# Four instead of three seven-product chunks in the first column-block pair of four late stages

## The chip, the cores and the metric

The kernel runs on one core of one Trainium2 chip. The metric is device time in microseconds (us) of one launch. Before the change it is 1014.27 us, the median of three runs (1013.76 to 1014.40).

## What is computed

One pre-norm layer on 256 tokens of width 2048, in float32, and a final norm. All large terms are products of a 256 x 2048 token matrix with a weight matrix that is read from memory once:

```python
h = rms_norm(x, norm_g)
proj = h @ w_in                      # 2048 x 20496, split into q k v o za gif xb zb ga gb
ya = mlstm_branch(...)               # 256 x 2048
yb = rglru_branch(...)               # 256 x 2048
ya, yb = ya @ w_branch_a, yb @ w_branch_b
merged = sigmoid(ga_p) * ya + sigmoid(gb_p) * yb
y = x + merged @ w_out
out = rms_norm(y, final_g)
```

## The kernel before, in words

**Precision.** Every operand is split in two float32r halves, `hi` (a rounded copy made by ScalarE, ACT) and `lo` (what is left, a subtraction by VectorE, DVE). A product of two operands is three matmuls: hi x hi, hi x lo, lo x hi. So each weight chunk that arrives must pass ACT and DVE before TensorE (PE) can use it: `load_chunk` (DMA L133, copy L140, subtraction L141).

**Chunks and pairs.** A weight matrix is cut in column blocks of 512 and in eight k chunks of 256 rows, `kq` 0 to 7; one chunk of one block is 128 x 1024 in SBUF (512 KB). Function `pair` (L171 to L266) computes two column blocks together, each 256 tokens x 512 columns. They stand in two PSUM tiles `acc` of two banks each; the pool for `acc` holds two tiles, so the next pair's first tile takes the place of this pair's first, and its second that of the second. A k chunk of a pair goes one of two ways:

- `plain` (L235): 2 blocks x 2 k tiles x 2 token tiles = 8 products = 24 matmuls with 512 columns. Two ACT copies (L140) and two DVE subtractions (L141), all 128 x 1024.
- `products` (L187): seven products in place of eight, 21 matmuls, by a Winograd scheme. The weight side needs sums: `t1` and `t2`, each by two DVE instructions of 128 x 512 (L199, L200, L203, L204); then four splits (L180, L181): one of 128 x 512 (`b`) and three of 128 x 1024. The token side needs four sums of 128 x 128 blocks, a "form", made once per chunk by `make_form`: L277 (128 x 512, joins hi and lo, left out where the whole value is at hand), L280 to L283 (128 x 128 each), L284 (ACT) and L285 (128 x 512).

Four of the seven products go to four single PSUM banks `aux`, called p1, p5, p7, p6; the other three go straight into the `acc` tiles. After the last products chunk the aux banks are folded into the result tiles `dst`: an ACT copy of p1 (L252), then DVE adds p6 (L253), p7 (L254) and p5 twice (L255, L256). The plain chunks that are still to come follow, those of the first block and then those of the second, and after each block DVE adds its `acc` tile to `dst` (L262), which frees that tile for the next pair.

**Places.** The tables `S_...` name the chunks of a pair that go by `products`, the tables `L_...` the places (0 to 7) at which they come in the sequence. Four late stages consist of two pairs each, p = 0 and p = 1: `WB` (yb times w_branch_b), `GB` and `GA` (the projections gb and ga of h), and `WA` (ya times w_branch_a). In all eight pairs it is chunks 0, 2, 4, at places 0, 2, 4 (1, 3, 5 in the second pair of `WA`). So after the last products chunk of a pair three plain places per block remain (two in the second pair of `WA`). After `WA` the stage `WO` (output projection) follows; its pair already has four products chunks at places 0, 2, 4, 6.

**Order and buffers.** The program is written straight down; a scheduler sorts the instructions of each engine, with `urgent()` marking those of the weight path. On the chip, each engine then goes through its own list in order, and an instruction that waits holds back all behind it. Arriving chunks have six buffers (`raw`), split weights four pairs (`whi`, `wlo`). Forms for `yb` stand in `PT` (slots 0 to 2), that of h chunk 2 in slot 3; those of h chunks 0 and 4 were made earlier in `F0` and `F4`. The form of ya chunk 0 goes to `PT` slot 0 after `WB`, those of ya chunks 2 and 4 to slots 1 and 2, written in the program after `GA`.

Of the kernel before, what the change touches and what calls it, by code (L numbers as in the profile page):

```python
# [10 lines left out]
F32R = mybir.dt.float32r  # L11
# [8 lines left out]
NB = 512  # L20
# [3 lines left out]
EPS = 1e-6  # L24
NEG = -1e30

S_WB, S_GB, S_GA, S_WA = [((0, 2, 4), (0, 2, 4))] * 4
S_OZ = (((4, 0), (2, 4)), ((4,), (1,)), ((4, 0), (2, 5)), ((4, 0), (0, 2)))
S_V = (((4,), (4,)), ((4,), (4,)))
S_WO = (0, 1, 2, 4)  # L30
L_WB, L_GB, L_GA, L_WA = ((0, 2, 4), (0, 2, 4)), ((0, 2, 4), (0, 2, 4)), ((0, 2, 4), (0, 2, 4)), ((0, 2, 4), (1, 3, 5))
L_WO = (0, 2, 4, 6)
H_FORMS = (4, 0)
PLAN = (dict(Y=('c0', '', '', 'c1',),
# [12 lines left out]
def f(ap):  # L47
    return ap.bitcast(F32)
# [3 lines left out]
def hybrid_encoder(ctx: ExitStack, tc: tile.TileContext, x, xt, pk, bif, fg, wg, wi, wr, wa, wb, wo, out):  # L52
# [12 lines left out]
    def name(n):  # L65
        uid[0] += 1
        return f"{n}_{uid[0]}"
# [4 lines left out]
    def sl(tag, dt=F32, cols=4096):  # L72
        return slot.tile([P, cols], dt, tag=tag, name=name("s" + tag))
# [41 lines left out]
    def drain():  # L115
        while queue or any(lanes):
            tick()
        lanes.clear()
# [149 lines left out]
    def halves(t, i):  # L268
        return t[:, i * 1024:i * 1024 + NB], t[:, i * 1024 + NB:(i + 1) * 1024]

    def make_form(fm, full=None, parts=None, temp=None):
        u = xp.rearrange("p a b -> p (a b)") if temp is None else temp
        if full is None:
            full = u[:, NB:2 * NB]
            hi, lo = parts
            v = full if len(hi.shape) == 2 else full.rearrange("p (k s) -> p k s", s=S)
            dve.tensor_add(v, f(hi), f(lo))  # L277
        a11, a21, a12, a22 = [full[:, i * P:(i + 1) * P] for i in range(4)]
        s1, s2, s3, s4 = [u[:, i * P:(i + 1) * P] for i in range(4)]
        dve.tensor_add(s1, a21, a22)  # L280
        dve.tensor_sub(s2, s1, a11)
        dve.tensor_sub(s3, a11, a21)
        dve.tensor_sub(s4, a12, s2)  # L283
        act.copy(fm[0], u[:, :NB])  # L284
        dve.tensor_sub(fm[1], u[:, :NB], f(fm[0]))  # L285
# [604 lines left out]
    yah, yal = Cols([yas["h"]], 4096), Cols([yas["l"]], 4096)  # L890
    ybh, ybl = [], []
    fslot = {}
    fm_t = []

    def form(x, kq, i, **kw):
        fslot[x, kq] = halves(fm_t[0], i)
        make_form(fslot[x, kq], **kw)

    def h_form(kq, i):
        form("h", kq, i, parts=h_parts(kq))  # L900

    def ya_form(kq, i):
        form("a", kq, i, parts=[t(kq * NB, (kq + 1) * NB) for t in (yah, yal)])

    def forms(x):
        return {kq: v for (n, kq), v in fslot.items() if n == x}
# [3 lines left out]

    k_yb, k_h, k_ya = (sorted(set(sum(v, ()))) for v in (S_WB, S_GB + S_GA, S_WA))
    k_h = [kq for kq in k_h if kq not in hf]
    early = [lambda kq=kq, i=i: h_form(kq, i) for kq, i in zip(k_h, (3, 0, 1))]
    early += [lambda kq=kq, i=i: ya_form(kq, i) for kq, i in zip(k_ya[:1], (3, 0, 1)[len(early):])]

    for j in range(4):
        for i in range(2):
            both = half_tr(wi[BLK_ZB + j], i)
            if i == 0:
                zt = hp.tile([P, 2 * NB], F32, tag="zz" if j else "vhi", name=name("zt"))  # L920
                sg = hp.tile([P, 2 * NB], F32, tag="to" if j else "vlo", name=name("sg"))
            fold(zt[:, i * NB:(i + 1) * NB], both)
        act.activation(sg, zt, AF.Silu)
        dve.tensor_mul(sg, sg, hs[:, j * 1024:(j + 1) * 1024])
        ybh.append(sl(f"C{j}", F32R, 1024))
        ybl.append(sl(f"D{j}", F32R, 1024))
        act.copy(ybh[j], sg)
        dve.tensor_sub(ybl[j], sg, f(ybh[j]))
        if j == 0:
            fm_t.append(sl("PT", F32R))  # L930
        if j == 0:
            drain()
        for kq in (2 * j, 2 * j + 1):
            if kq in k_yb:
                form("b", kq, k_yb.index(kq), full=sg[:, (kq % 2) * NB:(kq % 2 + 1) * NB])
        if j == 1:
            early[0]()
    ybh, ybl = Cols(ybh, 1024), Cols(ybl, 1024)
    nb11 = [0]

# [6 lines left out]
    sgv = [sgb[:, j * 1024:(j + 1) * 1024] for j in range(4)]  # L947
    for p in range(2):
        pair((wb[2 * p], wb[2 * p + 1]), ybh, ybl, forms("b"), S_WB[p], sgv[2 * p:2 * p + 2], b11, lambda jj: None, None, L_WB[p])
    for fn in early[1:]:  # L950
        fn()
    for p in range(2):
        gb = [sl(f"D{2 * p + i}", F32, 1024) for i in range(2)]

        def epi_gb(jj, p=p, gb=gb):
            act.activation(gb[jj], gb[jj], AF.Sigmoid)
            dve.tensor_mul(sgv[2 * p + jj], sgv[2 * p + jj], gb[jj])

        pair((wi[BLK_GB + 2 * p], wi[BLK_GB + 2 * p + 1]), hhi, hlo, forms("h"), S_GB[p], gb, b11, epi_gb, None, L_GB[p])
    ga = []  # L960
    for p in range(2):
        ga += [sl(f"C{2 * p + i}", F32, 1024) for i in range(2)]
# [2 lines left out]
            act.activation(ga[2 * p + jj], ga[2 * p + jj], AF.Sigmoid)  # L965

        pair((wi[BLK_GA + 2 * p], wi[BLK_GA + 2 * p + 1]), hhi, hlo, forms("h"), S_GA[p], ga[2 * p:], b11, epi_ga, None, L_GA[p])
    for i, kq in enumerate(k_ya[1:]):
        ya_form(kq, 1 + i)

    m_t = sl("HL", F32R, 8192)
    mh, ml = Cols([m_t[:, :4096]], 4096), Cols([m_t[:, 4096:]], 4096)
# [157 lines left out]
```

## Time and profile before

| | before |
|---|---|
| time, median of three runs | 1014.27 us |
| span of the profiled execution | 1012.2 us |
| PE busy | 1003.0 us (99%) |
| DVE busy | 875.8 us (87%) |
| ACT busy | 628.6 us (62%) |
| mean share of the DMA engines | 58.9% |
| mean granted TensorE clock | 0.998 |

The profile shows one execution, whose span runs from the first to the last instruction; the median of the runs is 2.07 us above that span, and this difference is taken as the time around it. Matmuls overlap in the pipeline: one is listed with 0.39 us, and in a steady row the next starts about 0.227 us later. A DVE row is likewise listed a little longer than its distance to the next. Times on a timeline are us from the start of the span.

### The profile page before, as it was taken

How to read it: one execution, taken by the hardware profiler on the slowest of the kernel's cores; microseconds unless marked ns; L12 is line 12 of the kernel's file. 1: busy time of each engine (PE TensorE's matmuls, PEld its weight loads, DVE VectorE, ACT ScalarE, POOL GpSimd, SP SyncE). 2: the span in 40 equal slices, each digit the busy share in tenths (PEclk: the TensorE clock that was granted, in tenths of full speed). 3: DMA queues.
4: the chain of work that ended last, by engine and by line, in shares of the span. 5: the costliest groups of instructions: out<-in, count | busy, mean ns of one | idle time of the engine just before them, and what ended most of it. 6: DMA issues, size and time to landing. Idle time of an engine off the chain costs nothing.

```text
span 1012.2 us, 13718 instructions
## 1 busy us (share of the span) xinstructions
PE 1003.0 (99%) x5045; PEld 853.2 (84%) x5045; DVE 875.8 (87%) x1167; ACT 628.6 (62%) x825; POOL 18.6 (2%) x37
## 2 busy tenths in 40 slices
PE   9999999999999999999999999999999999999997
PEld 9888988888888888888888888888888888888886
DVE  6687898889769888997697888998898988999996
ACT  7546477756695786667955564655655656455562
POOL 1000000001001000000100000000000000000000
PEclk9999999999999999999999999999999999999999
DMA  9765446565555565657466466666566656568452
GB/s 349 263 208 157 160 153 198 173 213 197 167 190 167 177 197 184 210 167 227 146 199 208 155 208 188 212 212 201 187 216 200 219 177 212 184 217 336 161 200 83
DMA packets 56387, 199.32 MB, mean 197 GB/s; under 512 B 6400, under 2 KB 7424, under 8 KB 55936
## 3 DMA queue, kind: packets, MB, share of 16 engines
q1 hardware_dynamic: 55456, 197.13, 58.9%
q10 hardware_dynamic: 864, 1.32, 0.4%
q8 instruction: 39, 0.64, 0.3%
q14 instruction: 28, 0.23, 0.1%
HBM read 196.33 MB, written 2.10 MB: 196 GB/s over the span
## 4 chain that ended last, share of the span: by engine, by line
PE 97%; DVE 1%; DMA 1%; ACT 0%; issue 0%; ACTq 0%; SPq 0%; DVEq 0%
PE acc L176 17%; PE acc L177 17%; PE acc L174 17%; PE acc L315 16%; PE acc L318 8%; PE aux L176 3%; PE aux L174 3%; PE aux L177 3%; PE aux L855 1%; PE aux L721 1%; PE aux L720 1%; PE aux L719 1%; PE aux L1053 1%; PE aux L1052 1%; PE aux L1051 1%; PE acc L156 1%
## 5 line engine op out<-in xcount | busy, mean ns | idle before, releaser
L140 ACT CAST whi<-raw 128x1024 fp32r<-128x1024 f32 (+1 forms) x284 | 294.8, 1046 | 196.0 <-PE acc L177 99.7
L141 DVE TENSOR_TENSOR wlo<-raw,whi 128x1024 fp32r<-128x1024 f32 (+1 forms) x284 | 341.5, 1213 | 76.2 <-ACT whi L140 74.4
L176 PE MATMUL acc<-wlo,sHL 128*128 128x512 f32 x554 | 215.9, 390 | 0.0
L177 PE MATMUL acc<-whi,sHL 128*128 128x512 f32 x554 | 215.8, 390 | 0.0
L174 PE MATMUL acc<-whi,sHL 128*128 128x512 f32 x554 | 213.3, 390 | 0.0
L315 PE MATMUL acc<-sHL,whi 128*128 128x512 f32 x704 | 175.9, 393 | 0.0
L315 PEld LDWEIGHTS acc<-sHL,whi 128*128 128x128 f32 x704 | 127.4, 189 | 23.5
L174 PEld LDWEIGHTS acc<-whi,sHL 128*128 128x128 f32 x554 | 104.0, 188 | 21.2
L176 PEld LDWEIGHTS acc<-wlo,sHL 128*128 128x128 f32 x554 | 104.1, 188 | 21.0
L177 PEld LDWEIGHTS acc<-whi,sHL 128*128 128x128 f32 x554 | 104.0, 188 | 20.9
L318 PEld LDWEIGHTS acc<-sHL,wlo 128*128 128x128 f32 x704 | 95.3, 190 | 6.0
L180 ACT CAST whi<-t 128x1024 fp32r<-128x1024 f32 x70 | 73.5, 1051 | 42.9 <-PE acc L177 13.9
L318 PE MATMUL acc<-sHL,wlo 128*128 128x256 f32 x704 | 99.0, 283 | 0.0
L181 DVE TENSOR_TENSOR wlo<-t,whi 128x1024 fp32r<-128x1024 f32 x70 | 85.5, 1222 | 9.0 <-ACT whi L180 8.5
L180 ACT CAST whi<-raw 128x1024 fp32r<-128x1024 f32 x37 | 39.0, 1053 | 27.6 <-PE acc L177 16.9
L181 DVE TENSOR_TENSOR wlo<-raw,whi 128x1024 fp32r<-128x1024 f32 x37 | 45.2, 1222 | 8.7 <-ACT whi L180 8.7
L180 ACT CAST b<-raw 128x512 fp32r<-128x512 f32 x28 | 17.4, 621 | 39.2 <-DMA raw<-wi 16.5
L176 PE MATMUL acc<-wlo,sC 128*128 128x512 f32 x92 | 35.9, 390 | 0.4 <-DVE wlo L141 0.4
L176 PE MATMUL acc<-wlo,sA 128*128 128x512 f32 x92 | 36.0, 392 | 0.0
L177 PE MATMUL acc<-whi,sD 128*128 128x512 f32 x92 | 35.8, 389 | 0.0
L177 PE MATMUL acc<-whi,sB 128*128 128x512 f32 x92 | 35.8, 389 | 0.0
L174 PE MATMUL acc<-whi,sC 128*128 128x512 f32 x92 | 35.3, 389 | 0.0
(361 smaller groups left out, 1589.1 us busy)
## 6 DMA issues: line engine op xcount, KB each, us to landing
raw<-wi SPq DMA_DIRECT2D x254, 512.0 KB, 4.2
raw<-wb SPq DMA_DIRECT2D x32, 512.0 KB, 4.1
raw<-wa SPq DMA_DIRECT2D x32, 512.0 KB, 4.0
raw<-wo SPq DMA_DIRECT2D x32, 512.0 KB, 4.8
raw<-wr SPq DMA_DIRECT2D x8, 512.0 KB, 4.0
sB<-x SPq DMA_DIRECT2D x4, 512.0 KB, 7.7
sA<-x SPq DMA_DIRECT2D x1, 2048.0 KB, 7.9
sA<-xt SPq DMA_DIRECT2D x7, 256.0 KB, 6.7
```

The costliest lines, as they stand in the source:

```text
L140: last_copy[0] = act.copy(hi[:, r], raw[:, r]).ins
L141: last_sub[0] = dve.tensor_sub(lo[:, r], raw[:, r], f(hi[:, r])).ins
L156: pe.matmul(ps[tb], a, wl, start=False, stop=False)
L174: pe.matmul(ps, a, wh, start=id(ps) not in began, stop=False)
L176: pe.matmul(ps, a, wl, start=False, stop=False)
L177: pe.matmul(ps, b, wh, start=False, stop=stop)
L180: act.copy(hi, v)
L181: dve.tensor_sub(lo, v, f(hi))
L315: pe.matmul(ps[m], hi[:, o:o + P], hl_t[:, 2 * k * S:2 * (k + 1) * S], start=(k == 0), stop=(turn and k == KT - 1), skip_group_check=True)
L318: pe.matmul(ps[m][:, :S], lo[:, o:o + P], hhi(k * S, (k + 1) * S), start=False, stop=(not turn and k == KT - 1), skip_group_check=True)
L719: pe.matmul(dst, whi[:, o:o + P], xh[:, r], start=True, stop=False)
L720: pe.matmul(dst, whi[:, o:o + P], xl[:, r], start=False, stop=False)
```

## The change

The first pair of each of the four stages gets a fourth products chunk, `kq` 6, at place 6. Only place 7 is left behind it. The token side then needs forms of chunk 6 of yb, h and ya, and the forms move: yb takes all four `PT` slots; both h forms (chunks 2 and 6) are written after `WB`, into slots 0 and 1; ya chunks 0 and 2 after the first and second pair of `GB`, into slots 2 and 3; ya chunks 4 and 6 after `GA`, into `F0` and `F4`. The early calls in the zb stage go. The host packs chunk 6 of those pairs as it packs the other products chunks.

```diff
-S_WB, S_GB, S_GA, S_WA = [((0, 2, 4), (0, 2, 4))] * 4
+S_WB, S_GB, S_GA, S_WA = [((0, 2, 4, 6), (0, 2, 4))] * 4
...
-L_WB, L_GB, L_GA, L_WA = ((0, 2, 4), (0, 2, 4)), ((0, 2, 4), (0, 2, 4)), ((0, 2, 4), (0, 2, 4)), ((0, 2, 4), (1, 3, 5))
+L_WB, L_GB, L_GA = [((0, 2, 4, 6), (0, 2, 4))] * 3
+L_WA = ((0, 2, 4, 6), (1, 3, 5))
...
-    early = [lambda kq=kq, i=i: h_form(kq, i) for kq, i in zip(k_h, (3, 0, 1))]
-    early += [lambda kq=kq, i=i: ya_form(kq, i) for kq, i in zip(k_ya[:1], (3, 0, 1)[len(early):])]
...
-        if j == 1:
-            early[0]()
...
-    for fn in early[1:]:
-        fn()
+    for i, kq in enumerate(k_h):
+        h_form(kq, i)
...
         pair((wi[BLK_GB + 2 * p], wi[BLK_GB + 2 * p + 1]), hhi, hlo, forms("h"), S_GB[p], gb, b11, epi_gb, None, L_GB[p])
+        ya_form(k_ya[p], 2 + p)
...
-    for i, kq in enumerate(k_ya[1:]):
-        ya_form(kq, 1 + i)
+    for kq, slot_ in zip(k_ya[2:], H_FORMS[::-1]):
+        fslot["a", kq] = halves(sl(f"F{slot_}", F32R, 1024), 0)
+        make_form(fslot["a", kq], parts=[t(kq * NB, (kq + 1) * NB) for t in (yah, yal)])
```

The scheduler's new order is shown at one boundary, that from the first to the second pair of `WB`; the other three have the same shape. Line numbers are one higher in the changed kernel here (L253 there is L252 before). The names: `sE` is the result tile of `WB`, `aux_...` are the banks p1, p5, p7, p6, `wlo` split weights, `t` the weight sums, `b` the split of 128 x 512, `raw` arrived chunks. DVE before, from the second fold (L254) on; the first fold, L253 on `aux_5588` (bank p6), and one L141 stand just ahead of it:

```order
L254 TENSOR_TENSOR sE_5557<-aux_5587,sE_5557 128x512
L141 TENSOR_TENSOR wlo_5817<-raw_5815,whi_5816 128x1024
L255 TENSOR_TENSOR sE_5557<-aux_5586,sE_5557 128x512
L256 TENSOR_TENSOR sE_5557<-aux_5586,sE_5557 128x512
L141 TENSOR_TENSOR wlo_5836<-raw_5834,whi_5835 128x1024
L199 TENSOR_TENSOR t_5898<-raw_5891 128x512
L181 TENSOR_TENSOR b_1260_5895<-raw_5891,b_1260_5895 128x512
L200 TENSOR_TENSOR t_5898<-raw_5892,raw_5891 128x512
L141 TENSOR_TENSOR wlo_5854<-raw_5852,whi_5853 128x1024
L203 TENSOR_TENSOR t_5899<-t_5898,raw_5891 128x512
L141 TENSOR_TENSOR wlo_5872<-raw_5870,whi_5871 128x1024
L204 TENSOR_TENSOR t_5899<-raw_5892,t_5899 128x512
```

The next instruction is the first `acc` addition, L262 on `acc_5558`. DVE in the changed kernel, up to the first `acc` addition; the first fold, L254 on `aux_5587` (bank p6), and one L205 stand just ahead of the piece:

```order
L182 TENSOR_TENSOR wlo_5912<-t_5907,whi_5911 128x1024
L255 TENSOR_TENSOR sE_5556<-aux_5586,sE_5556 128x512
L182 TENSOR_TENSOR b_1288_5990<-raw_5986,b_1288_5990 128x512
L200 TENSOR_TENSOR t_5993<-raw_5986 128x512
L201 TENSOR_TENSOR t_5993<-raw_5987,raw_5986 128x512
L182 TENSOR_TENSOR wlo_5918<-t_5908,whi_5917 128x1024
L256 TENSOR_TENSOR sE_5556<-aux_5585,sE_5556 128x512
L257 TENSOR_TENSOR sE_5556<-aux_5585,sE_5556 128x512
L182 TENSOR_TENSOR wlo_5922<-raw_5901,whi_5921 128x1024
L142 TENSOR_TENSOR wlo_5952<-raw_5950,whi_5951 128x1024
L204 TENSOR_TENSOR t_5994<-t_5993,raw_5986 128x512
L263 TENSOR_TENSOR sE_5556<-sE_5556,acc_5557 128x1024
```

Both `acc` additions now stand one behind the other (a second L263, on `acc_5558`, follows), and between the first fold and them stands work for the next pair's first two products chunks; before, there were also five of this pair's own plain chunks in between.

PE before at the same boundary, from the first pair's last matmul (into `acc_5559`) to the first that writes the next pair's tile `acc_5889`. That one stands 90 matmuls behind the last one into `aux_5588` (p6):

```order
L177 MATMUL acc_5559<-whi_5871,sD_1168_5554 128x512
L174 MATMUL aux_5917<-whi_5902,sPT_4955 128x512
L176 MATMUL aux_5917<-wlo_5903,sPT_4955 128x512
L177 MATMUL aux_5917<-whi_5902,sPT_4955 128x512
L174 MATMUL aux_5918<-whi_5902,sPT_4955 128x512
L176 MATMUL aux_5918<-wlo_5903,sPT_4955 128x512
L177 MATMUL aux_5918<-whi_5902,sPT_4955 128x512
L174 MATMUL aux_5919<-whi_5908,sPT_4955 128x512
L174 MATMUL acc_5889<-whi_5908,sC_1040_4951 128x512
```

PE in the changed kernel, the next pair's first matmuls up to the first that writes its tile `acc_5898`; that one stands 44 matmuls behind the last one into `aux_5587` (p6):

```order
L175 MATMUL aux_5928<-whi_5917,sPT_4955 128x512
L175 MATMUL aux_5927<-whi_5911,sPT_4955 128x512
L177 MATMUL aux_5927<-wlo_5912,sPT_4955 128x512
L178 MATMUL aux_5927<-whi_5911,sPT_4955 128x512
L177 MATMUL aux_5925<-b_1288_5990,sC_1083_5150 128x512
L178 MATMUL aux_5925<-b_1288_5990,sD_1084_5151 128x512
L177 MATMUL aux_5928<-wlo_5918,sPT_4955 128x512
L178 MATMUL aux_5928<-whi_5917,sPT_4955 128x512
L175 MATMUL aux_5926<-whi_5911,sPT_4955 128x512
L177 MATMUL aux_5926<-wlo_5912,sPT_4955 128x512
L178 MATMUL aux_5926<-whi_5911,sPT_4955 128x512
L175 MATMUL acc_5898<-whi_5917,sC_1040_4951 128x512
```

The matmuls between the last one of p6 and the first into the next pair's `acc` tile have become fewer by half, 44 in place of 90, mainly because two plain places (48 matmuls) no longer stand there.

## The prediction

> **What bounds the kernel now.** First the page: how busy each engine is, and what the chain of work that ended last consists of.
>
> ```profile
> span 1012.2 us, 13718 instructions
> PE 1003.0 (99%) x5045; PEld 853.2 (84%) x5045; DVE 875.8 (87%) x1167; ACT 628.6 (62%) x825; POOL 18.6 (2%) x37
> PE 97%; DVE 1%; DMA 1%; ACT 0%; issue 0%; ACTq 0%; SPq 0%; DVEq 0%
> ```
>
> PE sets the end: a matmul less is time less, as long as PE does not begin to wait. DVE is second, and 87% is a mean, so I read the late stages by themselves: the windows (columns: length, busy PE, weight loads, DVE, ACT, POOL, each with its count, then clock, DMA share, GB/s) and who PE waited for from 560 to 960 us.
>
> ```profile
> 598.00:925.00 327.00, 326.63 (x1453) 270.15 (x1452) 295.99 (x338) 181.70 (x194) 0.00 (x0) 1.00 0.63 210
> 598.00:640.00 42.00, 41.63 (x184) 34.12 (x183) 35.73 (x44) 22.05 (x25) 0.00 (x0) 1.00 0.58 192
> 640.00:682.00 42.00, 42.00 (x187) 34.79 (x186) 41.23 (x53) 23.16 (x26) 0.00 (x0) 1.00 0.67 218
> ```
>
> ```profile
> PE acc L176 <- DVE wlo L141: 0.4, 1, 0.4
> ```
>
> PE waits once in these four stages, for 0.4 us. DVE has 327.0 - 296.0 = 31.0 us of idle time there, but it is spread unevenly: 6.3 us in one window, 0.8 us in the next. ACT has half its time free.
>
> Next the rate of both engines, from the timelines at the boundary between the two pairs of `WB`. On PE these are the last matmul into the bank p6 and, 102 matmuls later in the order of before, the first into the second pair's second `acc` tile:
>
> ```profile
> 607.05 0.39 PE L177 MATMUL aux<-whi,sPT 128*128 128x512 f32 x1
> 630.17 0.39 PE L174 MATMUL acc<-whi,sPT 128*128 128x512 f32 x1
> ```
>
> 23.12 / 102 = 0.2267 us for each matmul, with no wait between. On DVE, from the last weight subtraction ahead of the folds to the second `acc` addition (first column start, second length):
>
> ```profile
> 606.11 1.23 DVE L141 TENSOR_TENSOR wlo<-raw,whi 128x1024 fp32r<-128x1024 f32 x1 [1.68 <-ACT whi L140]
> 607.90 0.69 DVE L253 TENSOR_TENSOR sE<-aux,sE 128x512 f32<-128x512 f32 x1 [0.56 <-PE acc L177]
> 608.51 1.22 DVE L141 TENSOR_TENSOR wlo<-raw,whi 128x1024 fp32r<-128x1024 f32 x1
> 609.64 0.68 DVE L254 TENSOR_TENSOR sE<-aux,sE 128x512 f32<-128x512 f32 x1
> 610.24 1.22 DVE L141 TENSOR_TENSOR wlo<-raw,whi 128x1024 fp32r<-128x1024 f32 x1
> ...
> 618.98 1.22 DVE L262 TENSOR_TENSOR sE<-sE,acc 128x1024 f32<-128x1024 f32 x1
> ...
> 628.61 1.21 DVE L262 TENSOR_TENSOR sE<-sE,acc 128x1024 f32<-128x1024 f32 x1
> ```
>
> From start to start, a DVE instruction of 128 x 1024 takes about 1.135 us (608.51 to 609.64), one of 128 x 512 takes 0.60 (609.64 to 610.24). The fold L253 begins 0.85 us after the last p6 matmul begins (607.90 - 607.05), and it waited for PE. The first L262 follows the fold by 11.08 us (618.98 - 607.90). With the fold, fourteen instructions stand ahead of it in DVE's order of before, five of 1.135 and nine of 0.60: 11.08. So the list runs without a gap there, and a sum over it gives its times.
>
> **What the change saves on PE.** One plain place is 24 matmuls, one products place 21. Four places change: 4 x 3 x 0.2267 = 2.72 us. The 0.4 us wait of before lies at a boundary that changes; I count it as gone too.
>
> **What it adds on DVE.** A plain place costs 2 x 1.135 = 2.27 us, a products place 3 x 1.135 + 5 x 0.60 = 6.41: 4.14 more, 16.6 for four. Forms are added for chunk 6 of h and ya (join and last subtraction of 0.60, four small sums) and of yb (no join). The small sums:
>
> ```profile
> 646.71 0.28 DVE L280 TENSOR_TENSOR xp<-xp 128x128 f32<-128x128 f32 x1
> 646.91 0.29 DVE L282 TENSOR_TENSOR xp<-xp 128x128 f32<-128x128 f32 x1
> ```
>
> 0.20 each, so 2.0 + 2.0 + 1.4 = 5.4 us. Together 22.0 us against 31.0 idle. By the sum it fits. ACT gets one copy of 128 x 512 and one of 128 x 1024 more per place, far below its free half. The DMA moves the same chunks. So what decides is where the work falls in DVE's list.
>
> **The boundary inside each stage.** After the change only one plain place is left behind the last products place. The second pair's first `acc` tile is free only when L263 has added the old one, and L263 stands in DVE's list behind the folds and behind weight work for the next pair. Behind the waiting PE instruction stands everything that PE has. I compare, from the start S of the last p6 matmul:
>
> - PE arrives after as many matmuls as stand between in the new order: `WB` 44, `GB` 47, `GA` 48, `WA` 44, times 0.2267: S + 9.97, 10.65, 10.88, 9.97.
> - DVE begins the first fold at S + 0.85 at the earliest and ends L263 after its list. `WB`: nine of 0.60 and five of 1.135 = 11.08; `GB`: eight and six = 11.61; `GA`: eight and five = 10.48; `WA`: seven and five = 9.88; each plus 0.08, since the last one counts with its length 1.22 and not its spacing. That is S + 12.01, 12.54, 11.41, 10.81.
>
> PE is there 2.04, 1.89, 0.53 and 0.84 us too early. The same sum on before: the first L262 ends at S + 13.14 (timeline: 618.98 + 1.22 - 607.05 = 13.15), while PE needs the tile 90 matmuls behind S, at 20.40; the second L262 ends at S + 20.1 by the sum and at 22.8 in the timeline, needed at 23.12. That boundary had 7 us to spare in one place and 0.3 in the other; now it is negative.
>
> In `WA` the second pair goes on badly: to the subtraction of its last products chunk's third weight split, DVE has 17 of 1.135 and 17 of 0.60 from the fold on, 29.5 + 0.93 = S + 30.4, and PE wants it after 123 matmuls and two groups of transposes, S + 28.8. I take 1.6 there in place of 0.84. In the other three stages the wait at the tile gives DVE the time for what follows (the tightest later need is short by 0.7 and 0.8 before that wait of 1.9 to 2.0). Least waits: 2.04 + 1.89 + 0.53 + 1.6 = 6.1 us, or 5.3 if `WA` gets by with 0.84.
>
> The waits can be longer, since DVE itself waits for ACT's copies and for chunks that arrive late:
>
> ```profile
> DVE wlo L181 <- ACT whi L180: 12.3, 15, 1.7
> DVE wlo L141 <- ACT whi L140: 11.5, 10, 1.7
> DVE b L181 <- ACT b L180: 2.9, 3, 2.2
> ```
>
> ```profile
> raw<-wb SPq DMA_DIRECT2D x32, 512.0 KB, 4.1
> ```
>
> In before the subtraction at 606.11 had waited for its copy, and ended 0.65 us ahead of the fold (606.11 + 1.14). In the new `WB` one L205 and one L142 more (1.735 us) stand between it and the fold: the list starts 1.1 us later. At the other boundaries no such pair stands there, and I take 0.4 as half of a possible 0.8. In the list itself `b` and two sums need raw chunks whose buffers come free only just before it, 4.1 us ahead of use: 0 to 0.7 us each. Taken: `WB` 2.04 + 1.1 = 3.1, `GB` 1.89 + 0.4 = 2.3, `GA` 0.9, `WA` 2.0, together 8.3 us. Upper end: `WB` 3.9, `GB` 2.8, `GA` 2.0, `WA` 2.4 = 11.1.
>
> The sum: -2.7 - 0.4 + 8.3 = +5.2 us. The span becomes 1017.4; the median of before lies 2.07 above its span (1014.27 - 1012.2), so 1019.5. Least waits give 1014.27 + 5.3 - 3.1 = 1016.5, the upper end 1022.3.
>
> One row can be read against a rule. Between the start of the last p6 matmul and the fold the row has 0.85 us. The Trainium skill ("TensorE: Matmul & The Clock Gate", section "Single matmul latency") gives a lone warm matmul of 512 columns about 0.38 us; by that alone each list could start 0.47 us sooner, an estimate that would take some 1.9 us off the four waits and bring the sum to +3.3. The trace's 0.85, which is from one matmul's start to the fold's start and so holds the signal as well, is what the sum above keeps.
>
> **The rivals.** *The gain arrives.* If the list keeps clear of PE, the time is 1014.27 - 2.7 - 0.4 = 1011.2. For it: PE has waited 0.4 us in all, and the sums fit into the idle 31 us. It decides at one point: L263 must end by S + 10, which needs 2 us of the split work in its list (two of 128 x 1024) to be done elsewhere; the list is fixed and the fold cannot begin before p6 ends. 0.10.
>
> *The waits cancel the gain.* If only `WB` waits much (about 3 us in all), 1014.3 comes out. For it: `GA` and `WA` are short by under a microsecond. 0.08.
>
> *DVE becomes the bound.* From the fold of `WB`'s first pair to that of `WA`'s second, DVE's new list, counted in the same way from fold to fold, sums to 31.2 + 50.9 + 30.0 + 49.2 + 29.1 + 45.7 + 39.5 = 275.6 us, PE's matmuls to about 283. 7 us is all that remains, where DVE was idle for 31, of which most ended by ACT's copies (12.3 + 11.5 + 2.9). If half of that idle time cannot be used, the stages take 275.6 + 15.5 = 291, 8 us over PE; with 3.1 off and some 5 us of boundary waits beside it, about +10: 1024. Against it: DVE mostly idles when it is ahead, at full buffers. 0.12.
>
> *The clock falls.* After the last matmuls the granted clock drops with PE's idleness:
>
> ```profile
> 1004.00:1008.00 4.00, 1.21 (x11) 1.00 (x9) 2.65 (x9) 1.02 (x2) 0.00 (x0) 1.00 0.01 5
> 1008.00:1012.00 4.00, 0.00 (x0) 0.00 (x0) 0.11 (x1) 0.00 (x0) 0.00 (x0) 0.62 0.72 257
> ```
>
> A boundary wait of 3 us or more could start this in mid-kernel: four microseconds at 0.62 lose 1.5 us of PE's work, so one or two such add 1.5 to 3.0: 1021 to 1022.5. The Trainium skill states it as a rule ("TensorE: Matmul & The Clock Gate", "What's actually happening"): half clock after an idle window of about 3.4 us. The clock 1.00 beside the wait of 0.4 us does not test it. 0.05.
>
> **How the numbers follow.** The forecast has 0.65, its own range is 1016.5 to 1022.3. A measurement of this kernel tells 0.2% from no change, 2.0 us: faster is below 1012.2, slower above 1016.3. Faster: 0.10. Same: 0.08 and 0.02 of the forecast's low end, 0.10. Slower: the rest, 0.63 + 0.12 + 0.05 = 0.80. The range leaves out the gain (0.10) and the far half of the DVE-bound case (0.06): 1014.0 to 1023.0.
>
> **What would show it.** Right: PE's list of waits names DVE's L263 four times, once per stage at the first matmul into a new `acc` tile, with 2 to 4 us in `WB` and `GB` and about 1 in `GA`; L263 stands twice in a row on DVE's timeline; `WA` shows PE waiting for `wlo`; PE's rows are fewer by 12. Wrong: PE without waits there and the span shorter by 3 us; PE waiting for `wlo` all through the stages with DVE busy near 100% (the DVE-bound case); a clock below 1.00 in a window between 600 and 930 us (the clock case).

## The result and the profile after

The change makes the kernel slower: 1030.24 us, median of four runs (1027.90 to 1031.82), against 1014.01 (1013.55 to 1014.40) for the kernel before on the same chip. The ratio is 1.0161, 95% interval 1.0147 to 1.0176. The prediction had the sign, not the size: 1019.5, with 1023.0 as the upper end. The profiled execution took 1030.09 us, its span is 1028.4.

The page after, in the same rows as before (span, busy time by engine, and the chain that ended last):

```profile
span 1028.4 us, 13751 instructions
PE 1009.0 (98%) x5033; PEld 852.8 (83%) x5033; DVE 897.1 (87%) x1208; ACT 635.2 (62%) x836; POOL 18.6 (2%) x37
PE 85%; DVE 8%; DMA 4%; issue 2%; ACT 1%; ACTq 0%; DVEq 0%; SPq 0%
```

Twelve matmuls fewer (5045 to 5033), and yet PE is listed 6 us busier: matmuls that run at a lower clock count longer, and the last one ahead of each gap counts with its listed 0.39 us in place of its spacing of 0.227. The chain, 97% PE before, now goes through DVE for 8% and through DMA for 4%. The windows of the four stages, of the 42 us around the boundary of `WB` and of the 42 us behind them (PE, weight loads, DVE, ACT, POOL; the third figure from the end is the clock):

```profile
598.00:925.00 327.00, 316.45 (x1365) 256.62 (x1364) 304.76 (x371) 181.71 (x197) 0.00 (x0) 0.98 0.58 196
598.00:640.00 42.00, 36.81 (x146) 28.05 (x145) 37.00 (x49) 18.36 (x21) 0.00 (x0) 0.92 0.61 200
640.00:682.00 42.00, 42.00 (x187) 34.76 (x186) 40.74 (x59) 23.64 (x26) 0.00 (x0) 1.00 0.49 164
```

The stretch around the boundary of `WB` loses most: 146 rows of PE where before had 184, at a mean clock of 0.92. And DVE still has 327.0 - 304.8 = 22.2 us of idle time, in stages in which PE waits for it. The list of PE's waits from 598 to 925 us (total, times, longest), where before had one of 0.4:

```profile
PE acc L175 <- DVE sE L263: 3.1, 1, 3.1
PE acc L175 <- DVE sD L263: 2.9, 1, 2.9
PE aux L177 <- DVE wlo L182: 1.8, 4, 0.7
PE aux L175 <- ACT b L181: 1.2, 1, 1.2
PE aux L175 <- DVE sE L257: 0.5, 1, 0.5
PE aux L175 <- ACT whi L181: 0.4, 1, 0.4
PE acc L175 <- DVE sC L263: 0.4, 1, 0.4
```

The first two and the last are the waits at the boundary for the old tile, in `WB`, `GB` and `GA`; the 1.2 is `WA`'s, for a split of `b` whose chunk came late. Start to start, beyond 0.2267, these four gaps are 3.29, 3.08, 0.57 and 1.39 us: together 8.3, the sum that the prediction took, though its parts differ (3.1, 2.3, 0.9 and 2.0 there), so that the agreement is partly luck. What it did not take stands around them. First PE at the boundary of `WB` (start, length, what it waited for):

```profile
627.72 0.74 PE L175 MATMUL aux<-whi,sPT 128*128 128x512 f32 x2 [0.44 <-ACT whi L181]
629.84 0.50 PE L177 MATMUL aux<-wlo,sPT 128*128 128x512 f32 x1 [0.45 <-DVE wlo L182]
631.03 0.50 PE L175 MATMUL aux<-whi,sPT 128*128 128x512 f32 x1 [0.47 <-DVE sE L257]
631.61 0.40 PE L178 MATMUL aux<-whi,sPT 128*128 128x512 f32 x1
635.13 0.77 PE L175 MATMUL acc<-whi,sC 128*128 128x512 f32 x1 [3.12 <-DVE sE L263]
635.69 0.63 PE L177 MATMUL acc<-wlo,sC 128*128 128x512 f32 x1
636.12 0.63 PE L178 MATMUL acc<-whi,sD 128*128 128x512 f32 x1
```

Three shorter waits precede the long one, and behind it the matmuls stand 0.43 us apart instead of 0.227: the clock is at a half. Windows of 1 us show where it falls and rises, in `WB` and in `GB`:

```profile
632.00:633.00 1.00, 0.00 (x1) 0.00 (x0) 1.00 (x2) 0.96 (x1) 0.00 (x0) 1.00 0.00 0
633.00:634.00 1.00, 0.00 (x0) 0.00 (x0) 1.00 (x3) 0.08 (x1) 0.00 (x0) 0.57 0.79 213
...
639.00:640.00 1.00, 1.00 (x4) 0.71 (x4) 0.75 (x2) 0.64 (x1) 0.00 (x0) 0.52 0.92 328
640.00:641.00 1.00, 1.00 (x6) 0.82 (x5) 0.97 (x2) 0.00 (x0) 0.00 (x0) 1.00 0.05 20
...
725.00:726.00 1.00, 1.00 (x5) 0.78 (x4) 1.00 (x2) 0.85 (x2) 0.00 (x0) 0.65 0.98 385
...
728.00:729.00 1.00, 1.00 (x5) 0.80 (x4) 1.00 (x2) 0.19 (x1) 0.00 (x0) 0.64 0.71 213
```

Then DVE on the way to that boundary: a wait for an arriving chunk (the products chunk at place 4 of `WB`'s first pair), and the list from the fold (L254) to the two `acc` additions (L263):

```profile
606.00 0.69 DVE L201 TENSOR_TENSOR t<-raw,raw 128x512 f32<-128x512 f32 x1 [2.07 <-DMA raw<-wb]
...
622.97 0.69 DVE L254 TENSOR_TENSOR sE<-aux,sE 128x512 f32<-128x512 f32 x1
...
626.75 0.69 DVE L182 TENSOR_TENSOR b<-raw,b 128x512 fp32r<-128x512 f32 x1 [0.76 <-ACT b L181]
...
633.76 2.35 DVE L263 TENSOR_TENSOR sE<-sE,acc 128x1024 f32<-128x1024 f32 x2
```

The last p6 matmul begins at 619.44:

```profile
619.44 0.40 PE L178 MATMUL aux<-whi,sPT 128*128 128x512 f32 x1
```

From the fold to the end of the first addition (length 1.22) are 633.76 + 1.22 - 622.97 = 12.01 us; without the 0.76 that DVE waited for `b`, 11.25, where the prediction's list has 11.16 (11.08 + 0.08). But the fold begins 3.5 us behind the last p6 matmul, where the prediction allowed 0.85 + 1.1. DVE comes to the boundary late, and one reason stands on its list of waits from 560 to 960 us:

```profile
DVE t L201 <- DMA raw<-wb: 3.7, 2, 2.1
DVE t L200 <- DMA raw<-wi: 2.7, 2, 1.4
...
```

From 598 to 925 us DVE waits 8.2 us for chunks (2.8 before), while its waits for ACT have halved (26.7 to 13.3). So three causes offer themselves: DVE's list at the boundary, late chunks, the clock. A fourth is DVE's load as a whole; if it were all, nothing could be regained by treating the other three.

### The profile page after: what moved, and what is told of

Same layout as the page of the kernel before. It is cut to its first block, busy times and chain, and to the rows that moved or that the text cites. A ratio compares the mean times of both kernels' runs of the same rounds, so it can differ in the third digit from the quotient of the medians.

```text
span 1028.4 us, 13751 instructions
## 1 busy us (share of the span) xinstructions
PE 1009.0 (98%) x5033; PEld 852.8 (83%) x5033; DVE 897.1 (87%) x1208; ACT 635.2 (62%) x836; POOL 18.6 (2%) x37
## 4 chain that ended last, share of the span: by engine, by line
PE 85%; DVE 8%; DMA 4%; issue 2%; ACT 1%; ACTq 0%; DVEq 0%; SPq 0%
PE acc L316 16%; PE acc L177 14%; PE acc L175 14%; PE acc L178 14%; PE acc L319 8%; PE aux L177 3%; PE aux L175 3%; PE aux L178 3%; DVE wlo L142 2%; DMA raw<-wi 2%; DMA raw<-wb 2%; DVE wlo L182 2%; PE aux L856 1%; PE aux L722 1%; PE aux L721 1%
## 5 line engine op out<-in xcount | busy, mean ns | idle before, releaser
L141 ACT CAST whi<-raw 128x1024 fp32r<-128x1024 f32 (+1 forms) x276 | 286.3, 1045 | 183.5 <-PE acc L178 85.9
L142 DVE TENSOR_TENSOR wlo<-raw,whi 128x1024 fp32r<-128x1024 f32 (+1 forms) x276 | 332.3, 1213 | 70.3 <-ACT whi L141 68.8
L175 PE MATMUL acc<-whi,sHL 128*128 128x512 f32 x542 | 209.6, 392 | 3.3 <-DVE sD L263 2.9
L177 PE MATMUL acc<-wlo,sHL 128*128 128x512 f32 x542 | 212.6, 392 | 0.1
L178 PE MATMUL acc<-whi,sHL 128*128 128x512 f32 x542 | 212.0, 391 | 0.0
L175 PEld LDWEIGHTS acc<-whi,sHL 128*128 128x128 f32 x542 | 102.1, 188 | 25.0 <-issue 3.3
L177 PEld LDWEIGHTS acc<-wlo,sHL 128*128 128x128 f32 x542 | 102.3, 189 | 21.6 <-DVE wlo L142 1.0
L178 PEld LDWEIGHTS acc<-whi,sHL 128*128 128x128 f32 x542 | 102.3, 189 | 20.6
L181 ACT CAST whi<-t 128x1024 fp32r<-128x1024 f32 x78 | 82.0, 1051 | 57.7 <-DVE t L205 23.1
L182 DVE TENSOR_TENSOR wlo<-t,whi 128x1024 fp32r<-128x1024 f32 x78 | 95.2, 1222 | 8.2 <-ACT whi L181 8.1
L181 ACT CAST whi<-raw 128x1024 fp32r<-128x1024 f32 x41 | 43.1, 1051 | 18.6 <-PE acc L178 8.1
L182 DVE TENSOR_TENSOR wlo<-raw,whi 128x1024 fp32r<-128x1024 f32 x41 | 50.1, 1222 | 2.0 <-ACT whi L181 2.0
L181 ACT CAST b<-raw 128x512 fp32r<-128x512 f32 x32 | 19.7, 619 | 51.7 <-DMA raw<-wi 20.6
L177 PE MATMUL acc<-wlo,sC 128*128 128x512 f32 x86 | 34.5, 401 | 0.0
L177 PE MATMUL acc<-wlo,sA 128*128 128x512 f32 x86 | 33.8, 393 | 0.0
```

What stands on the lines that cost most here:

```text
L141: last_copy[0] = act.copy(hi[:, r], raw[:, r]).ins
L142: last_sub[0] = dve.tensor_sub(lo[:, r], raw[:, r], f(hi[:, r])).ins
L175: pe.matmul(ps, a, wh, start=id(ps) not in began, stop=False)
L177: pe.matmul(ps, a, wl, start=False, stop=False)
L178: pe.matmul(ps, b, wh, start=False, stop=stop)
L181: act.copy(hi, v)
```

## The experiments

All times are medians; runs of the kernel before, taken together with each, have medians of 1013.5 to 1013.9, and the ratios are to these. "Lost" is a stretch's length less its matmuls at 0.2267 us (narrower ones in proportion); between 600 and 925 us before loses 1.6, the changed kernel 19.4.

**The forms alone.**

```diff
-S_WB, S_GB, S_GA, S_WA = [((0, 2, 4, 6), (0, 2, 4))] * 4
+S_WB, S_GB, S_GA, S_WA = [((0, 2, 4), (0, 2, 4))] * 4
```

(and the same in the `L_` tables)

> The fourth products chunk is taken back in all four stages (three chunks at the places of the kernel before); only the moved and re-slotted token-side sums of the change stay. Theory 1 (the loss is PE's waits at the boundary between the two pairs of a stage, the half clock behind them and the late weight splits ahead of them, all made by the fourth chunk at place 6): 1014 us, within 2 of the kernel before, no wait of PE above 0.5 us between 600 and 925 us, clock 1.00 there. Theory 2 (the fourth chunk's work makes DVE the bound in total, wherever it stands): 1014 too. Theory 3 (the moved sums hold up DVE's list at the boundaries): 1022 or more, with the waits for L263 or for weight splits still there.

1013.49, ratio 1.000 (0.9991 to 1.0009), no wait of PE in the stages. The moved sums cost nothing by themselves, so theory 3 is out for them; the added forms of chunk 6 are not in this run. Theories 1 and 2 both had 1014, and the run does not tell them apart.

**Other places.** `(0, 2, 4, 5)`, then `(0, 2, 3, 5)`, for `(0, 2, 4, 6)`.

> Four products chunks, the fourth at place 5 instead of 6, so that two plain places per block follow the last one; PE then has 24 matmuls, 5.4 us, more work between the last p6 matmul and the next pair's first acc tile (S + 15.4 to 16.3 us), and DVE two more splits of 1.135 us in the list ahead of L263 (at most S + 14.9). Theory 1: the waits for L263 (3.1, 2.9, 0.4) fall below 0.5 us each, the clock stays above 0.9, and the time falls by at least 9 us against the changed kernel, to 1014 to 1021; two products chunks in a row may add waits for weight splits of 1 to 2 us a stage. Theory 2: 1028 or more, since DVE has the same work and what PE does not wait for at L263 it waits for at the weight splits. Theory 3: 1028 or more, with the waits for L263 where they were.

> As place 5, but with the third products chunk at place 3 instead of 4 (places 0, 2, 3, 5), so that a plain place stands ahead of the last products chunk and lets DVE get ahead there. Theory 1: as with places 0, 2, 4, 5 or up to 3 us better, 1012 to 1020, with no wait for L263 above 0.5 us. Theory 2: 1028 or more. Theory 3: 1028 or more.

1023.80 (ratio 1.0087 to 1.0126) and 1021.34 (1.0059 to 1.0093). Both lie between the theories: 4 and 7 us below theory 2's 1028, 2.8 and 1.3 above the ranges of theory 1. With two plain places behind the last products chunk the waits for L263 shrink to 0.7 and to none, the clock is 1.00, and 6.4 and 8.9 us come back in all; but in the second PE still waits 2.3 for weight subtractions and 2.4 for ACT's copies. The boundary is one cause, not the only one.

**The tile freed by ACT.** ACT copies the `acc` tile to SBUF, DVE adds from the copy: first in every pair, then only in the four stages' first pairs.

```diff
-                dve.tensor_add(dst[jj], dst[jj], accs[jj])
...
+                act.copy(ta, accs[jj])
+                dve.tensor_add(dst[jj], dst[jj], ta)
```

> The changed kernel with places 0, 2, 4, 6, but in every pair ACT copies the acc tile to SBUF and DVE adds from there, so that the tile is free as soon as ACT has copied it and no longer where L263 stands in DVE's list. ACT gets 128 x 1024 copies of about 1 us, of which it has the time free. Theory 1: no wait of PE for L263, PE comes to the new tile at S + 10 to 11 and finds it free; the two falls of the clock to 0.5 go with the waits; of the 16 us the 8.3 at the boundaries and the 3.7 of clock come back unless PE meets the late weight splits of the second pair instead, so 1016 to 1023. Theory 2: the waits move to the weight splits (L182), the time stays above 1026. Theory 3: the same as theory 2.

> The copy of the acc tile by ACT only in the first pair of the four late stages (8 copies of 128 x 1024), not in the early stages, where it alone cost about 5.8 us in the run before it; DVE still adds, from the copy, and its total load is that of the changed kernel. Theory 1 (boundary waits, clock and late splits): 1019 to 1023, the late part of the run before without its early part, no wait for L263, clock 1.00 throughout. Theory 2 (DVE's total load is the bound, whichever wait shows it): 1026 to 1030, the waits move to the weight splits of the second pairs.

1027.66 (1.0121 to 1.0154) and 1025.69 (1.0103 to 1.0133), slower than theory 1 had them; the first lies where theory 2 had it, the second at the edge of it. The first run shows why it had to be done again: its folds stand 5.8 us late at 457 us, in the early stages, whose pairs it changes too. In the second no wait for L263 is left, and the clock is 1.00 in all four stages, but 15.3 us are lost where 19.4 were:

```profile
PE aux L177 <- DVE wlo L182: 1.9, 3, 0.9
PE aux L175 <- ACT whi L181: 1.5, 3, 0.7
...
```

All waits in this list sum to under 6; the rest are smaller gaps. PE no longer stops for long, and DVE's waits for chunks grew to 11.2 us. That PE now moves at DVE's pace is argued from these waits, not shown. A tile that is free earlier helps little while DVE stays late.

**GpSimd takes work from DVE.** It adds the copied tile; or it makes the two subtractions of place 7 in each first pair; or both.

```diff
...
-                last_sub[0] = dve.tensor_sub(lo[:, r], raw[:, r], f(hi[:, r])).ins
+                last_sub[0] = (sub or dve).tensor_sub(lo[:, r], raw[:, r], f(hi[:, r])).ins
...
```

> As the run before in this call, but GpSimd adds the copied acc tile to the result tile instead of DVE: the tile is freed by ACT as there, and DVE's load falls by 8 x 1.135 = 9.1 us. The difference between these two runs is DVE's load alone. Theory 1: less than 2 us between them, 1018 to 1022. Theory 2: most of the 9.1 us, 1011 to 1016, with the waits of PE for weight splits gone. A third possibility: GpSimd and DVE hold each other up, DVE's 128 x 1024 rows get longer than 1.23 us beside GpSimd's, and the time rises.

> The changed kernel, with DVE still adding the acc tiles, but the two weight subtractions of place 7 in the first pair of each of the four stages are made by GpSimd: 2.27 us less work in DVE's list ahead of L263, and 9.1 us less in all. This is the point that the prediction named as deciding for the gain. Theory 1: the waits at L263 of 3.3, 3.1, 0.6 and 1.4 us fall by 2.27 each, to 1.8 in all, and the clock stays at 1.00: 1030.2 - 6.6 - 3.7 = 1020. Theory 2: about the same 1020 to 1022, but with the waits for weight splits in the first pairs smaller too. New wait possible: PE for GpSimd's subtraction, if that takes over 3 us a tile; then 1025 or more.

> Both: the acc tile copied by ACT and added by GpSimd, and the two subtractions of place 7 made by GpSimd, in the first pair of the four stages; DVE is 18.2 us lighter, 3.8 above its load in the kernel before. Theory 1: 1013 to 1018, no wait at the boundary, small waits for splits in the first pairs. Theory 2: 1011 to 1013, the gain of 2.7 us arrives, since DVE's load is that of the kernel before. If GpSimd's instructions take over 3 us each, PE or the second pair's tiles wait for GpSimd: 1020 or more.

1035.16, 1028.41 and 1045.06 (ratios 1.0208, 1.0142, 1.0305). The third possibility of the first run came true: GpSimd and DVE hold each other up (PE itself waits for GpSimd only 0.6 us in the second run). In the second run, at the boundary of `WB`, GpSimd's two subtractions and DVE beside them:

```profile
619.10 6.17 POOL L142 TENSOR_TENSOR wlo<-raw,whi 128x1024 fp32r<-128x1024 f32 x2 [114.44 <-DVE wlo L182]
```

```profile
620.13 2.88 DVE L204 TENSOR_TENSOR t<-t,raw 128x512 f32<-128x512 f32 x1
622.93 0.68 DVE L254 TENSOR_TENSOR sE<-aux,sE 128x512 f32<-128x512 f32 x1
623.53 2.28 DVE L205 TENSOR_TENSOR t<-raw,t 128x512 f32<-128x512 f32 x1
```

Rows of 0.69 take 2.88 and 2.28; the fold between them, which has an operand in PSUM, takes 0.68. DVE is 898.5 us busy in all with 9.1 us less to do, where the changed kernel had 897.1: its other rows grew by some 10.5. These runs therefore say nothing about DVE's load.

**`WB` alone with four.**

> The fourth products chunk in WB alone; GB, GA and WA as in the kernel before. The trace of the changed kernel puts 8.2 us of its loss into WB, 5.8 into GB, 0.7 into GA, 1.6 into WA, each with 0.7 saved. If each stage's loss is made in it, 1013.8 + 8.2 = 1022. If DVE, behind in WB, passes its lateness on to the next stages, 1023 to 1026; if it catches up at the expense of nothing, the second-pair folds of GB to WA stand as late as that of WB.

1021.81 (1.0057 to 1.0088), as 1022 expected. Behind `WB` the folds of all later stages stand 4.3 to 5.6 us late in the profile, with no growth (its execution, 1019.02, was the fastest of four). Each stage makes its own loss.

**The waits filled.** Thirteen matmuls by zeros ahead of the waiting one in `WB`, twelve in `GB`.

```diff
+            if kq == seq[0]:
+                for _ in range(fill):
+                    pe.matmul(p6, zr, h2[:, lf], start=False, stop=False)
...
```

> The changed kernel with 13 matmuls by a tile of zeros (512 columns, into an aux bank that is still being summed, to which they add nothing) ahead of the waiting matmul in WB, and 12 in GB. They fill 2.9 and 2.7 us of the waits of 3.3 and 3.1, so that PE is hardly idle there; the tile comes free when it did. If the clock falls because PE idles, it stays at 1.00 in both places and the 3.7 us of matmuls at 0.427 us come back: 1026.5. If the clock has another cause, or its price is made up by a later wait, 1029.5 to 1030.5.

1026.58 (1.0115 to 1.0149): 3.7 us come back from added work (3.3 against the run below that holds the same move of small tiles and nothing else). Windows behind the two boundaries, where the clock had been 0.50:

```profile
636.00:638.00 2.00, 2.00 (x10) 1.65 (x9) 2.00 (x2) 1.01 (x2) 0.00 (x0) 1.00 0.61 248
...
722.00:724.00 2.00, 2.00 (x10) 1.66 (x9) 1.28 (x2) 1.99 (x2) 0.00 (x0) 1.00 0.38 154
```

So the half clock follows from PE's idleness. Its price fits the changed kernel's trace, where 20 matmuls at half clock start some 0.2 us further apart, 3.9 us in all.

**A seventh chunk buffer.** With the changed places, and with `(0, 2, 3, 5)`. Room for it came from moving eight small early tiles, a move that was then run alone.

```diff
-            raw = wp.tile([P, KC * NB], F32, tag="raw", name=name("raw"), bufs=6)
+            raw = wp.tile([P, KC * NB], F32, tag="raw", name=name("raw"), bufs=7)
...
```

> The changed kernel with seven instead of six buffers for arriving chunks; nothing else moves. In the changed kernel DVE waits 8.2 us in the four stages for chunks that arrive late (2.8 in the kernel before), and each such wait pushes all that stands behind it, the tile that L263 frees included. Theory 4 (the lateness that the prediction left out comes from chunks whose buffer comes free too late): those waits fall below 3 us, the boundary waits shrink with them, 1020 to 1025. Theory 1 without it (boundary waits are DVE's list alone): 1028 to 1030, since the list is the same.

> Places 0, 2, 3, 5 for the four products chunks and seven buffers for arriving chunks. With six buffers these places gave 1021.3, with waits of PE for weight splits of 9 us in all. Theory 4: 1013 to 1018, DVE's waits for chunks below 3 us. Theory 2 (DVE's work is the bound there): 1020 to 1022, no change by the buffer. A time below 1011.5 would be better than the kernel before and needs all waits gone.

> The changed kernel with nothing but the move of eight small early tiles to another place in SBUF, which made room for the seventh buffer. If the seventh buffer is what helped: 1030, as the changed kernel. If the move did: 1022, and the fall of the time in the run that fills PE's waits would be in doubt as well, since it holds the same move.

1021.94 (1.0057 to 1.0093), 1022.58 (1.0072 to 1.0103), and 1029.83 (1.0145 to 1.0175) for the move alone. So 8 us of the loss go with one more buffer; DVE's waits for chunks fall from 8.2 to 1.0, and DVE begins the fold of `WB` 2.05 us behind the last p6 matmul (620.23 to 622.28), no longer 3.5. At places 0, 2, 3, 5 the buffer does not help (1021.34 before, 1022.58 now), though those waits fall there too, from 6.4 to 3.3. There theory 4 missed, and theory 2, which had no change by the buffer, was right: with the boundary relieved and fewer late chunks some 8.7 us are still lost, and DVE's work as the bound is not excluded for them.

**Two subtractions less in DVE's list.** In each first pair the two at place 7, with six and with seven buffers. These kernels leave out the lo half of those chunks, so their result lacks it; they serve to measure.

```diff
...
-                last_sub[0] = dve.tensor_sub(lo[:, r], raw[:, r], f(hi[:, r])).ins
-        return hi, lo
+                if not skip:
+                    last_sub[0] = dve.tensor_sub(lo[:, r], raw[:, r], f(hi[:, r])).ins
+        return hi, hi if skip else lo
...
```

> The changed kernel without the two weight subtractions of place 7 in the first pair of the four stages (the lo half of those chunks is left out, the matmuls read the hi half in its place): 2.27 us less in DVE's list ahead of L263, and nothing given to another engine. Theory 1: the boundary waits of 3.3, 3.1, 0.6 and 1.4 us fall to 1.0, 0.8, 0 and 0, and no wait is long enough for the clock to fall: 1030.2 - 6.6 - 3.7 = 1020. Theory 2 (DVE's total load): the same 9.1 us less work, 1021. If chunks that arrive late decide instead: 1025 or more, with DVE's waits for raw chunks still at 8 us.

> The same, and with seven buffers for arriving chunks. If DVE's list at the boundary and late chunks are all that the prediction's rival of the arriving gain lacked, the gain arrives: 1011 to 1013, no wait of PE above 0.5 us between 600 and 925, clock 1.00. If DVE's load in total binds: 1015 or more, small waits for weight splits all through the first pairs.

1020.80 (1.0055 to 1.0085), as theory 1 had it, but theory 2's 1021 fits as well. DVE's waits for chunks are still 7.0 there. With seven buffers they fall to 0.3, and the time to 1016.00 (1.0012 to 1.0031): the late chunks still cost 4.8 us with the shorter list. Most of the loss is gone, but there is no gain, and the time lies where the expectation put it if DVE's load binds (1015 or more).

**A plain chunk first behind the boundary.** Second pairs of `WB`, `GB`, `GA` at `(1, 3, 5)`.

> The changed kernel with the second pairs of WB, GB and GA at places 1, 3, 5 as in WA: a plain chunk comes first behind the boundary, so DVE's list up to L263 (WB: eight of 0.60 and five of 1.135, 10.5 us, ends at S + 11.4) is 0.6 shorter, PE still comes to the tile after some 45 matmuls (S + 10.2). Theory 1: the waits for L263 fall to 1 to 2 us, the clock stays: 1022 to 1026. If the place of the second pair's products does not matter: 1029 to 1031.

1028.87 (1.0131 to 1.0170), no help. The wait changes its name, as in `GB`:

```profile
716.32 0.50 PE L175 MATMUL aux<-b,sHL 128*128 128x512 f32 x1 [2.57 <-ACT b L181]
```

DVE's waits for chunks from 598 to 925 us are 15.2 us here, the most of all runs.

**The seventh buffer from `WB` on,** without and with the two subtractions left out (every seventh chunk goes to a tile of its own).

> The changed kernel with a seventh buffer for chunks from WB on (every seventh chunk goes there); the stages ahead keep six. The run with seven from the start lost 19.4 - 9.4 = 10 us less than the changed kernel between 600 and 925 us (elapsed time less matmuls at 0.2267) and 3 us more ahead of them. If the early loss comes from the seventh buffer in the early stages: 1030.2 - 10 = 1020. If it comes with any seventh buffer: 1022 as before.

> The same, and without the two subtractions of place 7 in each first pair (the lo half of these chunks is left out, the matmuls read the hi half in its place). With seven buffers from the start this lost 2.5 us more than the kernel before between 600 and 925 us, against 2.7 saved, and some 2 us ahead of them. If the early loss is gone and the small waits in the four stages stay: 1013 to 1014, no change. If those waits were made by the early lateness: 1011 to 1012, the gain.

1021.72 (1.0064 to 1.0095) and 1014.81 (1.0001 to 1.0019). The first is no better than seven from the start (1021.94), the second 1.2 us better (1016.00 there); only there does the early lateness show in the median. Of the four executions of the first, the profiled one took 1018.88 us at a mean clock of 0.998, the others 1021.41 to 1022.10 at 0.993 to 0.996, so part of its median is clock that this trace does not show. What PE still waits for from 598 to 925 us, in the first run:

```profile
PE acc L181 <- DVE sD L269: 2.3, 1, 2.3
PE aux L181 <- ACT b L187: 2.1, 1, 2.1
PE aux L181 <- DVE sE L263: 0.8, 1, 0.8
PE acc L181 <- DVE sC L269: 0.4, 1, 0.4
```

and in the second:

```profile
PE aux L182 <- ACT whi L188: 1.0, 1, 1.0
PE acc L184 <- DVE wlo L149: 0.5, 1, 0.5
PE aux L184 <- DVE wlo L189: 0.4, 1, 0.4
```

With late chunks gone the waits for the old tile in `GB` and `GA` (L269) remain, near what the prediction took (2.3 and 0.9; measured 2.3 and 0.4). In `WB` PE does not wait for the tile any more, but 0.8 for a fold (L263 here) and 2.1 for the split of `b`, both just ahead of it. With the list shortened as well no boundary wait is left, and yet 5.1 us are lost from 600 to 925 where before lost 1.6: 3.5 us in small gaps against 2.7 saved, about +0.8. The median says +1.0. The gain does not arrive even then.

## Why the prediction was wrong

- **Saved on PE, 2.7 us: right in count,** twelve matmuls fewer. No run shows it as time; the last one is closest.
- **DVE's added work: right.** DVE is 21.3 us busier (875.8 to 897.1), 22.0 predicted.
- **DVE's list at the boundary: right.** Counted from where the fold begins, it takes 11.25 us in `WB` without the wait for `b` (11.16 worked out), 11.69 in `GB` (712.74 to 724.43; 11.69) and 10.56 in `GA` (798.54 to 809.10; 10.56). L263 stands twice in a row, and PE waits for it at the named place in `WB`, `GB` and `GA`. Leaving two rows of that list out brought 9.4 us (clock included); that run takes the same work from DVE's load, though, and does not tell the two apart. In `WA` the wait came at ACT's split of `b`, neither at L263 nor at `wlo`.
- **The step that failed: the start of the list, "`WB` 2.04 + 1.1 = 3.1", and within it "0 to 0.7 us each" for late chunks.** Only the wait at the tile is 3.3. In `WB` DVE began the fold 3.5 us behind p6 instead of 1.95 (in `GB` 1.90 instead of 1.25), and waited 0.76 more for `b`. PE, due at S + 9.97 = 629.4, got the tile at 635.1: 5.7 us, of which 2.4 are spread over waits for splits ahead of it. The prediction put the price of late chunks into the list as a small addition. In fact they make DVE late for the whole boundary: a buffer comes free only when DVE has read it (from 560 to 960 us the queue that fetches chunks waits 172.3 us in 25 waits for DVE's subtraction L182), so a late DVE makes the next chunk late, which makes DVE later. One buffer more brought back 8.3 us (the move of small tiles alone: 0.4), and with it the fold of `WB` begins 2.05 us behind p6, close to the 1.95 of the prediction. Of the 19.4 us lost between 600 and 925, the four gaps of the sum are 8.3 and the half clock 3.9; eight other waits of 0.2 to 0.9 us are 4.3, which the sum put at nothing, and gaps below 0.2 us 2.7 (1.6 before).
- **The second step that failed: the clock at 0.05, as a rival.** It was no rival but a consequence of the forecast's own numbers: 3.1 us of wait was taken for `WB`, and "a boundary wait of 3 us or more" was its condition. The clock fell in `WB` and in `GB`, and cost some 3.7 us, above the 1.5 to 3.0 named. Behind the rows: the Trainium skill ("TensorE: Matmul & The Clock Gate", section "What's actually happening") speaks of free-running windows of 3413 ns; the trace agrees, see below. The idle window of about 3.4 us that the prediction took over as a rule is longer than the gaps of 3.29 and 3.08 us that sufficed here, and the measurement decides.
- **"DVE becomes the bound", 0.12: not the whole loss; for the remainder open.** With the same work on DVE the seventh buffer alone brought 8.3 us back and the places 0, 2, 3, 5 alone 8.9, and DVE has 22 us idle after the change, so its load does not make the whole loss. But two times came out where the load had them (1022.58 and 1016.00, above), the runs that shorten the list also lighten the load, and the GpSimd runs that were to separate the two could not. Even in the two best runs some 2 to 3.5 us of small gaps remain. That they come from a DVE nearly full is argued from its waits, not shown.
- **The sum.** Loss by the medians 16.2 us. From the changed kernel, the longer buffer row alone gives 8.3 to 8.5, the shorter list alone 9.4, both 15.4 (1030.24 - 1014.81): they overlap by about 2.4. The clock is in both: the traces have 10.2 us of half clock in the four stages for the changed kernel, 3.4 and none with the longer buffer row, none with the shorter list. 1.0 is left, which with the 2.7 saved makes 3.7 that PE still loses.
- **"0.85" from p6 to the fold: misread, without consequence here.** The row of before names another matmul as what the fold waited for (`acc` L177), and the last such one ahead of the fold began only 0.40 earlier (607.50 to 607.90). Where the fold did wait for p6's last matmul, as in `GA` with two subtractions less and seven buffers, it began 0.43 behind that matmul's start. The row of before, then the two of that run:

```profile
607.50 0.39 PE L177 MATMUL acc<-whi,sD 128*128 128x512 f32 x1
...
787.30 0.39 PE L179 MATMUL aux<-whi,sPT 128*128 128x512 f32 x1
787.73 0.69 DVE L255 TENSOR_TENSOR sC<-aux,sC 128x512 f32<-128x512 f32 x1 [1.75 <-PE aux L179]
```

  So the other reading, the 0.38 us of the Trainium skill ("TensorE: Matmul & The Clock Gate", section "Single matmul latency"), was nearer. In the changed kernel DVE comes to the folds from its own list and waits for p6 at none of these boundaries, so the difference changes nothing there.

## What to carry to other kernels

When a change lets one engine fall behind, the waits it adds at the tightest point are not the whole price: count also what that engine's lateness delays through the buffers that it must free, and ask of every predicted wait of about 2 us or more what the TensorE clock will do. A list of work that just fits between two events has to be counted from when the engine gets there, not from when it could. Before giving another engine a share of a full one, look at whether the two can run side by side.

## What the runs showed of the hardware

**Half clock comes on a grid of 3.41 us.** In the windows above the clock falls at 633.14 (0.57 = 0.14 + 0.5 x 0.86) and is back at 639.96, 6.82 us; in `GB` it falls at 725.30 and is back at 728.72, 3.42. The two falls lie 92.16 us apart, 27.0 x 3.413. So a wait's length alone does not decide. In the run with filled waits, a gap of 2.08 us in `WA` was followed by 3.4 us of half clock:

```profile
885.00:886.00 1.00, 0.09 (x1) 0.09 (x1) 1.00 (x2) 0.76 (x2) 0.00 (x0) 1.00 0.90 360
886.00:887.00 1.00, 1.00 (x3) 0.81 (x4) 1.00 (x2) 0.81 (x1) 0.00 (x0) 0.65 0.48 193
...
889.00:890.00 1.00, 1.00 (x4) 0.77 (x4) 1.00 (x2) 0.18 (x1) 0.00 (x0) 0.64 0.00 0
```

A gap of 2.73 us, in the run with second pairs at 1, 3, 5, was not:

```profile
714.00:715.00 1.00, 0.00 (x0) 0.00 (x0) 1.00 (x3) 0.00 (x0) 0.00 (x0) 1.00 0.74 258
715.00:716.00 1.00, 0.00 (x0) 0.00 (x0) 1.00 (x2) 0.36 (x1) 0.00 (x0) 1.00 1.06 381
716.00:717.00 1.00, 0.68 (x3) 0.58 (x4) 1.00 (x3) 0.49 (x2) 0.00 (x0) 1.00 0.83 336
```

The first gap fell into one step of the grid (882.89 to 886.30). The second was shared by two: in that run the clock falls elsewhere, at 803.91, and 26 steps of 3.413 us earlier is 715.16, in the middle of the gap. In all traces here, each fall in the four stages follows a step of its run's grid in which PE, by the listed lengths of its matmuls, was idle for about half of the time or more; after steps with 0.43 or less idle there is none, and near one half both occur (0.51 ahead of the fall in `WB`; 0.55 without one, at 626 us in the run with second pairs at 1, 3, 5).

**GpSimd and DVE stop each other.** DVE rows of 0.69 us with both operands in SBUF took 2.3 to 2.9 us beside GpSimd's subtractions, and a row with one operand in PSUM took its usual 0.68. The Trainium skill ("SBUF — State Buffer", section "SBUF: two separate sides") gives this as an exclusive lock between a DVE operation with two SBUF inputs and a GpSimd operation that reads SBUF; the rows agree. Eight such subtractions, 21.0 us of GpSimd, cost DVE 10.5 us more than its other rows' usual time, against 9.1 saved.
